# Pairing a large and a small expert per slot in a routed expert stage, with one weight load issued before the size decision

## The chip, the cores and the metric

One core of one Trainium2 chip runs the whole program. The metric is the device time of one execution in microseconds (us). Five engines work beside each other, each with its own instruction stream and its own sequencer that takes branches: TensorE (PE in the rows, with PEld for its weight loads and PEldq for its sequencer), VectorE (DVE), ScalarE (ACT), GpSimd (POOL) and SyncE (SP). SP only issues transfers and takes branches; its instructions appear as SPq.

## The reference

The program is two transformer blocks of two layers each, on 256 latent tokens of width 1024 and 256 context tokens. Each layer of the first block has a mixture of experts, and only this part is touched. Layer 0 routes 512 tokens, layer 1 routes 256:

```python
g_idx = top-1 of 4 groups;  top_i = top-2 of the 8 experts of that group
experts = g_idx * EXPERTS_PER_GROUP + top_i            # 32 experts, 2 per token
counts = jnp.bincount(e_flat, length=N_EXPERTS)        # tokens of each expert
def expert_block(a):
    xb, e = a
    return (jax.nn.silu(xb @ w1[e]) * (xb @ w3[e])) @ w2[e]
y = sum over a token's two experts of weight * expert_block(token)
```

`w1` and `w3` are 1024x512 and `w2` is 512x1024, all float32, so one expert's weights are 6 MB. How many experts are used, and how many tokens each gets, is only known at run time. On these inputs the reference's routing gives layer 0 fifteen used experts with 216, 165, 139, 138, 118, 80, 58, 53, 29, 18, 4, 3, 1, 1 and 1 tokens, and layer 1 fourteen with 133, 119, 79, 61, 56, 24, 12, 9, 8, 6, 2, 1, 1 and 1.

## The kernel before

`route_tokens` (line 764) computes, on VectorE and TensorE, the size of each expert, a rank for each (`rn`), and from the rank a slot number `uc`. It writes small tables: `meta` and `meta2` hold the expert of each slot and its token count, `gtab` the token rows of each slot for the gathers, `stabs` the rows for the scatters. Two chosen experts stand in slots 0 and 1, so that their weights can be loaded ahead.

`experts` (line 982) is one long unrolled program of turns, one per slot, with branches that every engine takes for itself on a value that it has loaded from `meta2`:

- Two turns of kind "any" for slots 0 and 1.
- Then rounds (`round_`, line 1173). Round i has a "large" turn for slot 2 + i, counted from the large end, and a "small" turn for slot 31 - i, counted from the smallest used expert up. Large means more than 64 tokens. Layer 0 has a large turn in rounds 0 to 14, layer 1 in rounds 0 to 6. Each turn stands in `If n > 0` (line 1180); where the slot is empty, the Else only transposes the rows for the next turn (`next_rows`, line 1183).
- A turn of up to 32 tokens runs a quarter block, one of 33 to 64 a half block, one of more a full block of 128 rows and, over 128 tokens, a `rest` for the further rows (line 1167, behind a branch with a prefetch hint for TensorE). Each block is a first part (w1 and w3), the transposes of the next turn's rows (line 995), and a second part (w2), then a scatter on GpSimd (line 1000).
- Ahead of a turn, `ahead` issues a gather of token rows for a later turn on GpSimd (line 722).

With the sizes above, the executed experts of layer 0 come in the order 165, 118, 216, 1, 139, 1, 138, 1, 80, 3, then 4, 18, 29, 53 and 58, each of these five behind an empty large turn: five empty turns in all, for slots 6 to 10. Layer 1 runs 61, 79, 133, 1, 119, 1, then 1, 2, 6, 8 and 9 each behind an empty large turn (slots 4 to 8), and then 12, 24 and 56, which stand in rounds without a large turn.

Weights come in six pieces of 1 MB per expert (`expert_weights`, line 977; the transfer is line 143), issued by SP, inside the `If` of the turn. They go to a ring of buffers that is handed out in program order over the unrolled turns: 16 pieces in layer 0, 18 in layer 1. Empty turns have their places in the ring too. A piece's issue waits until the turn that used its buffer has left its branch, and until the transfer before it on the same completion counter is done. After the last turn, `combine` (line 1194) loads the scattered rows back (`y`, line 1202).

Of the kernel before, what the change touches and what calls it, by code (L numbers as in the profile page):

```python
# [11 lines left out]
I32 = mybir.dt.int32  # L12
# [85 lines left out]
class Builder:  # L98
# [665 lines left out]
    def route_tokens(self, l, nt, gp, mp, rp):  # L764
# [11 lines left out]
        units = mt([NE, 2 * NE], "units")  # L776
        nc.vector.tensor_copy(units[:, 0:NE], self.iota[0:NE, 0:NE])
        nc.vector.tensor_scalar(units[:, NE:], self.iota[0:NE, 0:NE], -1.0, float(NE - 1), ALU.mult, ALU.add)
# [76 lines left out]
        rn = mt([NE, 2], "rn")  # L855
        nc.vector.tensor_reduce(rn[:, 0:1], before, AX.X, ALU.add)
        used = mt([NE, NE], "used")
        nc.vector.tensor_scalar(used, srow, 0.0, None, ALU.is_gt)
        nc.vector.tensor_reduce(rn[:, 1:2], used, AX.X, ALU.add)
        few = mt([NE, 1], "few")  # L860
        nc.vector.tensor_scalar(few, size, 64.0, None, ALU.is_le)
        nc.vector.tensor_scalar(rn[:, 1:2], rn[:, 1:2], -1.0, float(NE), ALU.mult, ALU.add)
        uc = mt([NE, 1], "uc")
        nc.vector.scalar_tensor_tensor(uc, few, rn[:, 1:2], rn[:, 0:1], ALU.mult, ALU.add)
        uh = mt([NE, 2 * NE], "uh")
        nc.vector.tensor_scalar(uh, units, uc, None, ALU.is_equal)
# [7 lines left out]
        nc.tensor.matmul(mb[0:NE, 0:2 * NE], lhsT=eix, rhs=uh, start=True, stop=True)  # L874
        mb2 = self.bankB()
        nc.tensor.matmul(mb2[0:NE, 0:2 * NE], lhsT=cnt, rhs=uh, start=True, stop=True)

        meta = keep([1, 4 * NE], "meta", I32)
        nc.vector.tensor_copy(meta[:, 0:2 * NE], mb[0:1, 0:2 * NE])
        nc.vector.tensor_copy(meta[:, 2 * NE:4 * NE], mb2[0:1, 0:2 * NE])  # L880
# [38 lines left out]
        for out, parts in ((tb, self.iota[:, 0:P]), (sb, self.cst[:, C_IOTAM:C_IOTAM + P]),  # L919
# [13 lines left out]
            if out is tb:  # L933
                tx = rows_of(tb)
                gx = mt([P, GC], "gx")
                nc.vector.tensor_scalar(gx, tb, float(T), float(T), ALU.is_gt, ALU.mult)
                gtab = keep([P, GC], "gtab", I32)
                nc.vector.scalar_tensor_tensor(gtab, tx, -1.0, gx, ALU.add, ALU.subtract)

                meta2 = keep([1, 7 * NE], "meta2", I32)  # L940
                for i in range(2):
                    c = slice(2 * NE * i, 2 * NE * i + 2 * NE)
                    nc.vector.scalar_tensor_tensor(meta2[:, c], gtab[0:1, 0:2 * NE], 0.0, meta[:, c], ALU.mult, ALU.add)
                for i, op in enumerate((ALU.is_gt, ALU.is_le)):
                    v = meta2[:, (2 + i) * NE:(3 + i) * NE]
                    nc.vector.scalar_tensor_tensor(meta2[:, (4 + i) * NE:(5 + i) * NE], v, 64.0, v, op, ALU.mult)
                nc.vector.tensor_tensor(meta2[:, 6 * NE:7 * NE - 2], meta2[:, 4 * NE + 2:5 * NE],
                                        meta2[:, 5 * NE:6 * NE - 2], ALU.add)
# [33 lines left out]
    def experts(self, l, nt, mp, first, meta, meta2, gtab, stabs, XG, XE, ybuf):  # L982
# [121 lines left out]
        turns = [("any", 0, 0), ("any", 1, 1)]  # L1104
        for i in range(NE - 2):
            turns += [("large", i, 2 + i)] * (i < most[0]) + [("small", i, NE - 1 - i)]

        def ahead(k):
            if k + AHEAD < len(turns):
                kind, _, slot = turns[k + AHEAD]  # L1110
                gather(slot * nt, XG[k % AHEAD], 64 if kind == "small" else P)

        def turn(k, n, W):

            kind, i, slot = turns[k]
            x = XT[k % 2]
            groups = nt if kind == "any" else 1 + sum(i < m for m in most[1:nt]) if kind == "large" else 1

            def block(g, size, b=lambda: None):
# [4 lines left out]
                two(slot * nt + g, W, ht)  # L1124

            def rest(g):
# [3 lines left out]
                if more:  # L1130
                    with tc.If(load(meta2 if k > 1 else meta, 2 * NE + slot, T, engines=[ENG.Pool]) > P * (g + 1)):
                        gather(slot * nt + g + 1, XE)
# [14 lines left out]
            label = f"rest{l}_{k}"  # L1147
            if groups > 1:
                tc.mark_branch_hint_location(label, "LikelyTaken", [ENG.PE])
                with tc.If(load(meta2 if k > 1 else meta, 2 * NE + slot, T, engines=[ENG.Pool]) > P):  # L1150
                    gather(slot * nt + 1, XE)
            if kind == "large":
                block(0, 0, lambda: next_rows(k))
            else:
                with tc.If(n < 33) as fewer:
                    block(0, 2, lambda: next_rows(k))
                with fewer.Else():
                    if kind == "small":
                        block(0, 1, lambda: next_rows(k))
                    else:  # L1160
                        with tc.If(n < 65) as few:
                            block(0, 1, lambda: next_rows(k))
                        with few.Else():
                            block(0, 0, lambda: next_rows(k))
            if groups > 1:
                with tc.If(n > P, label=label):
                    rest(1)

        def next_rows(k):
            if k + 1 < len(turns):  # L1170
                rows_T(XG[(k + 1) % AHEAD], XT[(k + 1) % 2], 64 if turns[k + 1][0] == "small" else P)

        def round_(i):

            for k in [k for k, t in enumerate(turns) if k > 1 and t[1] == i]:
                kind, _, slot = turns[k]
                ahead(k)
                at, e = (4 * NE + slot, slot) if kind == "large" else (5 * NE + i, NE + i)
                n = load(meta2, at, T)
                with tc.If(n > 0) as some:  # L1180
                    turn(k, n, self.expert_weights(wm, load(meta2, e, NE - 1, engines=[ENG.SP])))
                with some.Else():
                    next_rows(k)
            if i + 1 < NE - 2:
                with tc.If(load(meta2, 6 * NE + i + 1, 2 * T) > 0):
                    round_(i + 1)

        for k in range(2):
            ahead(k)
            turn(k, load(meta, 2 * NE + k, T), first[k])  # L1190
        with tc.If(load(meta2, 6 * NE, 2 * T) > 0):
            round_(0)
# [557 lines left out]
```

## Time and profile before

| quantity | value |
|---|---|
| median of 3 runs | 2325.05 us (2316.84 to 2331.53) |
| the profiled execution | 2326.15 us, its span 2324.3 us |
| mean granted TensorE clock | 0.912 |
| busy share of the span | TensorE 84%, VectorE 43%, ScalarE 32%, GpSimd 12% |
| DMA, mean over the span | 196 GB/s |
| 390 to 800 us (layer 0: routing tables and experts) | TensorE busy 304 of 410 us, clock 0.86, DMA share 0.62, 241 GB/s |
| 1035 to 1337 us (layer 1: the same) | TensorE busy 200 of 302 us, clock 0.83, DMA share 0.73, 287 GB/s |

In timeline rows a time in brackets is how long the engine sat idle before the row's first instruction, and what released it; "issue" means that it waited for nothing that the profile shows.

### The profile page before, as it was taken

The numbers are of one execution on the slowest core, as the hardware profiler recorded it, in microseconds if no ns is written. First come the engines' busy times: TensorE is split into PE (matmuls) and PEld (weight loads), VectorE is DVE, ScalarE is ACT, GpSimd is POOL, SyncE is SP. The second block draws the span as 40 slices with busy tenths as digits, with TensorE's granted clock in tenths as the row PEclk, the third lists the DMA queues.
The fourth block names the chain that finished last, engine by engine and source line by source line (L and its number), as shares of the span: only waits on it lengthen the run. The fifth ranks groups of instructions, "written<-read, shape, count | busy, mean of one in ns | idle before, by whom it ended". The sixth has DMA issues, their size and how long they took to land. (4 is left out here: it accounts for less than half of the span.)

```text
span 2324.3 us, 27711 instructions
## 1 busy us (share of the span) xinstructions
PE 1948.4 (84%) x10138; PEld 1348.4 (58%) x10138; DVE 1002.8 (43%) x1956; ACT 739.9 (32%) x1322; POOL 272.6 (12%) x214
## 2 busy tenths in 40 slices
PE   6999796778876489977865549999899899998997
PEld 3656575334433167753432237777688677776885
DVE  3346655300000174561000056656654567566554
ACT  2233431100111154411111045444444355434442
POOL 0002301101111052120111102000200020002000
PEclk9999797789997789978987769999999999998998
DMA  9974115354767762156668764344455434454550
GB/s 396 375 280 155 65 37 217 130 209 187 317 255 296 276 239 70 42 205 273 242 253 340 307 241 169 129 145 168 163 186 185 152 129 147 143 181 150 184 181 29
DMA packets 75147, 456.01 MB, mean 196 GB/s; under 512 B 13544, under 2 KB 14092, under 8 KB 24496
## 3 DMA queue, kind: packets, MB, share of 16 engines
q1 hardware_dynamic: 61632, 430.99, 49.5%
q0 software_dynamic: 9664, 14.79, 1.8%
q10 hardware_dynamic: 3632, 7.37, 0.9%
q8 instruction: 129, 2.11, 0.4%
q14 instruction: 90, 0.74, 0.1%
HBM read 455.65 MB, written 13.30 MB: 202 GB/s over the span
## 5 line engine op out<-in xcount | busy, mean ns | idle before, releaser
L167 DVE TENSOR_TENSOR whl<-w,whl 128x1024 fp32r<-128x1024 f32 x312 | 397.1, 1287 | 234.9 <-ACT whl L166 224.2
L166 ACT ACTIVATE whl<-w 128x1024 fp32r<-128x1024 f32 x332 | 344.4, 1057 | 260.5 <-PE bankA L180 208.0
L178 PE MATMUL bankA<-whl,x2h 128*128 128x512 f32 (+1 forms) x864 | 345.3, 400 | 9.6 <-ACT x2h L238 7.2
L180 PE MATMUL bankA<-whl,x2l 128*128 128x512 f32 (+1 forms) x864 | 345.0, 400 | 5.8 <-DVE x2l L239 5.8
L179 PE MATMUL bankA<-whl,x2h 128*128 128x512 f32 (+1 forms) x864 | 342.0, 397 | 0.0
L178 PEld LDWEIGHTS bankA<-whl,x2h 128*128 128x128 f32 x864 | 168.4, 195 | 43.8 <-ACT x2h L238 8.2
L180 PEld LDWEIGHTS bankA<-whl,x2l 128*128 128x128 f32 x864 | 167.4, 194 | 40.6 <-DVE x2l L239 7.2
L179 PEld LDWEIGHTS bankA<-whl,x2h 128*128 128x128 f32 x864 | 167.9, 194 | 35.0 <-issue 2.0
L1071 PE MATMUL bankA<-w,xt 128*128 128x512 f32 x320 | 153.1, 641 | 17.2 <-issue 14.7
L1018 PE MATMUL bankA<-w,xt 128*32 128x256 f32 x1216 | 97.3, 463 | 55.5 <-DMA w<-in_wmoe 32.2
L178 PE MATMUL bankA<-whl,xh 128*128 128x512 f32 (+1 forms) x336 | 132.5, 395 | 5.4 <-ACT xh L238 5.4
L179 PE MATMUL bankA<-whl,xh 128*128 128x512 f32 (+1 forms) x336 | 129.4, 385 | 5.1 <-DVE whl L167 5.1
L180 PE MATMUL bankA<-whl,xl 128*128 128x512 f32 (+1 forms) x336 | 127.8, 384 | 0.1
L414 ACT ACTIVATE p<-bankS,sm 128x256 f32<-128x256 f32 (+2 forms) x160 | 85.7, 537 | 117.6 <-DVE sm L405 59.4
L1071 PEld LDWEIGHTS bankA<-w,xt 128*128 128x128 f32 x320 | 65.0, 206 | 99.7 <-issue 98.3
L213 POOL TENSOR_TENSOR sm<-sm,mhalf 128x1 f32<-128x1 f32 (+3 forms) x32 | 32.2, 1006 | 690.9 <-DVE sm L211 679.3
L1018 PEld LDWEIGHTS bankA<-w,xt 128*32 128x32 f32 x1216 | 47.7, 131 | 102.7 <-issue 44.7
L1022 DVE TENSOR_TENSOR s<-s,bankA 64x256 f32<-64x256 f32 x19 | 8.0, 423 | 221.9 <-ACT s L1021 221.9
L1000 POOL DMA_INDIRECT ybuf<-ys,stab x34 | 34.6, 1019 | 523.6 <-ACT ys L1038 147.1
L1075 DVE TENSOR_TENSOR s<-s,bankA 128x512 f32<-128x512 f32 x10 | 6.9, 688 | 195.2 <-PE bankA L1071 181.7
L178 PEld LDWEIGHTS bankA<-whl,xh 128*128 128x128 f32 x336 | 64.2, 191 | 32.0 <-ACT xh L238 7.4
L995 PE MATMUL bankB<-cst,xg 128*128 128x128 f32 (+1 forms) x328 | 40.4, 271 | 49.8 <-issue 31.6
(456 smaller groups left out, 2982.2 us busy)
## 6 DMA issues: line engine op xcount, KB each, us to landing
w<-in_wmoe SPq DMA_DIRECT2D x174, 1024.0 KB, 12.4
w<-in_wd SPq DMA_DIRECT2D x166, 1024.0 KB, 5.1
w<-in_wmod SPq DMA_DIRECT2D x48, 1024.0 KB, 7.5
y<-ybuf SPq DMA_DIRECT2D x12, 512.0 KB, 7.7
w<-in_rows SPq DMA_DIRECT2D x5, 1024.0 KB, 4.7
w<-mrow SPq DMA_DIRECT2D x7, 512.0 KB, 8.7
fbuf<-w SPq DMA_DIRECT2D x4, 512.0 KB, 2.8
nb<-in_nabias POOLq DMA_DIRECT2D x16, 128.0 KB, 2.5
```

Source lines behind the costliest of these rows:

```text
L166: nc.scalar.activation(h, s, AF.Copy)
L167: self.low = (eng or nc.vector).tensor_tensor(lo, s, h, ALU.subtract).ins
L178: mm(out, lhsT=xh, rhs=wh, start=start, stop=False)
L179: mm(out, lhsT=xh, rhs=wl, start=False, stop=False)
L180: mm(out, lhsT=xl, rhs=wh, start=False, stop=stop)
L213: self.power = self.nc.gpsimd.tensor_tensor(r, t, self.mhalf[:, :n], ALU.pow).ins
L414: nc.scalar.activation(p[:, :n], s[i][:, :n], AF.Exp, bias=nm[:, i:i + 1], accum_out=ss[:, i:i + 1])
L995: nc.tensor.transpose(xb[:, k], xg[0:rows, (4 * i + k) * P:(4 * i + k + 1) * P], self.ident[0:rows, 0:rows])
L1000: nc.gpsimd.indirect_dma_start(out=ybuf.rearrange("r (m d) -> (r m) d", m=1 << parts), out_offset=bass.IndirectOffsetOnAxis(ap=stabs[parts ...
L1018: nc.tensor.matmul(acc[r:r + 32], lhsT=xT[:, k, 0:32], rhs=wslice(W, m, k, 256 * f, 256), start=k == 0, stop=k == KT - 1)
L1022: nc.vector.tensor_tensor(s, s, acc[64:128], ALU.mult)
L1071: nc.tensor.matmul(acc[m], lhsT=xT[:, k], rhs=wslice(W, m, k), start=k == 0, stop=k == KT - 1)
```

## The change

The slot table is built another way, and the turns follow it.

- In the table, every used expert gets its place in the order in which it runs: slots 2, 4, 6, ... are the first, slots 3, 5, 7, ... the second of a pair. A large expert and a small one share a pair while there are large ones; the remaining small ones fill the pairs two by two. On these inputs the order in which the experts run is the same as before, in slots 0 to 14 in layer 0 and 0 to 13 in layer 1. An expert of no tokens gets a slot number beyond the table. The chain of small VectorE operations between `before` and `uc` has 17 operations where it had 5; the two operations that made `units` and four behind `gtab` are gone.
- The first of a pair has no `If n > 0`: its weight transfers stand straight in SP's stream. Its blocks stand behind one decision `either` (65 tokens): the Then side is `small` (quarter or half block), the Else side is `large` (full block and rest). The "any" turns of slots 0 and 1 use the same form.
- The second of a pair is only ever small, and keeps `If n > 0` and its Else. Inside it stands a prefetch hint for TensorE that the next pair's `either` is likely taken, that is, to `large`. Slot 2 has no hint.

```diff
+        r, u, b, s, few, near, uc, t = (mt([NE, 1], f"slot{i}") for i in range(8))
+        nc.vector.tensor_reduce(r, before, AX.X, ALU.add)
+        for c, n in ((0.0, u), (64.0, b)):
+            over = mt([NE, NE], "over")
+            nc.vector.tensor_scalar(over, srow, c, None, ALU.is_gt)
+            nc.vector.tensor_reduce(n, over, AX.X, ALU.add)
         nc.vector.tensor_scalar(few, size, 64.0, None, ALU.is_le)
-        uc = mt([NE, 1], "uc")
-        nc.vector.scalar_tensor_tensor(uc, few, rn[:, 1:2], rn[:, 0:1], ALU.mult, ALU.add)
+        nc.vector.tensor_tensor(s, u, r, ALU.subtract)
+        nc.vector.tensor_tensor(t, s, b, ALU.subtract)
+        nc.vector.tensor_scalar(near, t, -1.0, None, ALU.is_lt)
...
+        nc.vector.scalar_tensor_tensor(uc, t, few, uc, ALU.mult, ALU.add)
+        nc.vector.tensor_scalar(t, size, 0.0, float(4 * NE), ALU.is_equal, ALU.mult)
+        nc.vector.tensor_tensor(uc, uc, t, ALU.add)
...
+            if kind == "small":
+                small()
             else:
-                with tc.If(n < 33) as fewer:
-                    block(0, 2, lambda: next_rows(k))
+                with tc.If(n < 65, label=f"either{l}_{k}") as fewer:
+                    small()
                 with fewer.Else():
...
+                    large()
...
-        def round_(i):
-
-            for k in [k for k, t in enumerate(turns) if k > 1 and t[1] == i]:
-                kind, _, slot = turns[k]
-                ahead(k)
-                at, e = (4 * NE + slot, slot) if kind == "large" else (5 * NE + i, NE + i)
-                n = load(meta2, at, T)
-                with tc.If(n > 0) as some:
-                    turn(k, n, self.expert_weights(wm, load(meta2, e, NE - 1, engines=[ENG.SP])))
-                with some.Else():
-                    next_rows(k)
-            if i + 1 < NE - 2:
-                with tc.If(load(meta2, 6 * NE + i + 1, 2 * T) > 0):
-                    round_(i + 1)
+        def pair(k):
+
+            ahead(k)
+            turn(k, sized(k), load(meta2, NE + k, T), self.expert_weights(wm, load(meta2, k, NE - 1, engines=[ENG.SP])))
+            ahead(k + 1)
+            n = load(meta2, NE + k + 1, T)
+            with tc.If(n > 0) as some:
+                W = self.expert_weights(wm, load(meta2, k + 1, NE - 1, engines=[ENG.SP]))
+                if k + 2 < NE and sized(k + 2) == "large":
+                    tc.mark_branch_hint_location(f"either{l}_{k + 2}", "LikelyTaken", [ENG.PE])
+                turn(k + 1, "small", n, W)
+            with some.Else():
+                next_rows(k + 1)
+            if k + 2 < NE:
+                with tc.If(load(meta2, NE + k + 2, T) > 0):
+                    pair(k + 2)
```

On SP, at the end of a large turn of the kernel before (line 1166 is the end of its rest, line 1180 its Else and then the next turn's `If n > 0`, line 143 the weight pieces):

```order
L1166 UNCONDITIONAL_BRANCH
L1180 UNCONDITIONAL_BRANCH [waits SP_sequencer_49,DMAHW2_49,DMAHW3_49,DMAHW4_49,DMAHW5_49,DMAHW6_49,DMAHW7_49]
L1094 TENSOR_LOAD meta_3280
L1180 COMPARE_AND_BRANCH
L1094 TENSOR_LOAD meta_3280
L143 ISA
L143 DMA w<-in_wmoe 128x2048 [waits DMAHW3_49,DMAHW2_49,PE_49]
```

And in the changed kernel, at the end of the second turn of a pair (line 1186 is its Else, line 1194 the test whether there is a further pair) and the start of the next pair:

```order
L1186 UNCONDITIONAL_BRANCH [waits SP_sequencer_49,DMAHW0_49,DMAHW1_49,DMAHW2_49,DMAHW3_49,DMAHW4_49,DMAHW5_49]
L1096 TENSOR_LOAD meta_3295
L1194 COMPARE_AND_BRANCH
L1096 TENSOR_LOAD meta_3295
L143 ISA
L143 DMA w<-in_wmoe 128x2048 [waits DMAHW0_49,PE_49]
...
L143 DMA w<-in_wmoe 128x2048 [waits DMAHW5_49]
L1096 TENSOR_LOAD meta_3295
L1175 COMPARE_AND_BRANCH
L1167 COMPARE_AND_BRANCH
```

The Else with waits on the completion counters (DMAHW) of the weight transfers stood behind every turn; now it stands only behind the second of a pair. The first of a pair issues its six pieces right behind the test for the pair, and its size branch (line 1175) comes after them.

On TensorE, at the start of slot 2 in the kernel before (line 1191 tests for rounds, line 1180 is `If n > 0`, line 995 the transposes of the next turn's rows, which the scheduler has laid ahead of the full block, line 1071 the full block's matmuls):

```order
L1191 COMPARE_AND_BRANCH
L1094 TENSOR_LOAD meta_3280
L1180 COMPARE_AND_BRANCH
L1746 BRANCH_PREFETCH_HINT
L995 MATMUL bankB<-cst,xg_0_3072 128x64 [waits DVE_49,DMASW7_49,PE_49,Activation_49]
L1150 UNCONDITIONAL_BRANCH
...
L1071 MATMUL bankA<-w,xt_0_3377 128x512 [waits DMAHW2_49]
L1071 MATMUL bankA<-w,xt_0_3377 128x512 x3
```

And in the changed kernel, at the same slot (line 1200 tests for pairs, line 1175 is `either`, line 1167 the test for 33 tokens, 1020 a quarter block's matmul, 1073 a full block's):

```order
L1200 COMPARE_AND_BRANCH
L1096 TENSOR_LOAD meta_3295
L1175 COMPARE_AND_BRANCH
L1167 COMPARE_AND_BRANCH
L1020 MATMUL bankA<-w,xt_0_3388 32x256 [waits DVE_49,PE_49,DMAHW2_49,Activation_49]
...
L1167 UNCONDITIONAL_BRANCH
L1755 BRANCH_PREFETCH_HINT
L1073 MATMUL bankA<-w,xt_0_3388 128x512 [waits DVE_49,DMAHW2_49,PE_49,Activation_49]
L1159 UNCONDITIONAL_BRANCH
```

A full block stood next behind the test of its turn; now the code of a quarter and of a half block lies between the test and the full block, and a branch at line 1175 leads over them.

## Rows read from the trace of the kernel before

**Rows 1.** Stretches of both expert stages: window, us, engines' busy time (instructions), PEclk, DMA share, GB/s.
```profile
1200.00:1260.00 60.00, 31.08 (x362) 15.84 (x350) 2.15 (x6) 8.56 (x21) 10.98 (x11) 0.80 0.81 316
1260.00:1330.00 70.00, 43.84 (x378) 17.92 (x378) 3.26 (x8) 5.39 (x15) 6.84 (x7) 0.78 0.89 355
```

**Rows 2.** Waits of SP's sequencer (SPq), whole run: us in total, times, longest us.
```profile
SPq L1180 <- SPq L1180: 138.8, 49, 7.6
```

**Rows 3.** The sequencers at line 1180: count, duration ns min/median/max, first and last start us.
```profile
L1180 PEldq COMPARE_BRANCH  x35: 65/68/6523, 508.5 to 1309.3; - x35
L1180 POOLq INC_SWDGE_SEM  x10: 1142/1726/2305, 695.9 to 1258.2; - x10
```

**Rows 4.** Weight loads that SP issues: start us, duration us, pieces; last, issue to landing.
```profile
657.96 0.87 SPq L143 DMA_DIRECT2D w<-in_wmoe  x2
...
682.72 9.37 SPq L143 DMA_DIRECT2D w<-in_wmoe  x6
...
769.99 7.55 SPq L143 DMA_DIRECT2D w<-in_wmoe  x6
...
1173.26 3.81 SPq L143 DMA_DIRECT2D w<-in_wmoe  x6
...
1255.65 3.65 SPq L143 DMA_DIRECT2D w<-in_wmoe  x6
...
1261.85 45.76 SPq L143 DMA_DIRECT2D w<-in_wmoe  x18
...
w<-in_wmoe SPq DMA_DIRECT2D x174, 1024.0 KB, 12.4
```

**Rows 5.** TensorE at the end of layer 0's experts: start us, us, [idle before <-releaser].
```profile
683.89 3.66 PE L1018 MATMUL bankA<-w,xt 128*32 128x256 f32 x64 [1.30 <-DVEq L1166]
689.23 1.93 PE L1035 MATMUL bankA<-w,ht 128*32 128x256 f32 x32 [0.38 <-DVE ht L1028]
...
697.52 1.09 PE L995 MATMUL bankB<-cst,xg 64*128 64x64 f32 x8 [6.35 <-issue]
...
707.19 1.93 PE L1035 MATMUL bankA<-w,ht 128*32 128x256 f32 x32 [0.38 <-DVE ht L1028]
...
761.32 9.27 PE L1046 MATMUL bankA<-w,xt 128*64 128x512 f32 x30 [5.43 <-SPq L1180]
...
778.29 1.07 PE L1046 MATMUL bankA<-w,xt 128*64 128x512 f32 x2 [1.02 <-ACT xt L997]
...
790.33 3.65 PE L1061 MATMUL bankA<-w,ht 128*64 128x512 f32 x16 [0.52 <-DVE ht L1055]
```

**Rows 6.** TensorE at the end of layer 1's experts, same columns.
```profile
1145.83 1.93 PE L1035 MATMUL bankA<-w,ht 128*32 128x256 f32 x32 [0.38 <-DVE ht L1028]
...
1174.45 3.66 PE L1018 MATMUL bankA<-w,xt 128*32 128x256 f32 x64 [1.31 <-DVEq L1166]
...
1261.85 1.07 PE L1018 MATMUL bankA<-w,xt 128*32 128x256 f32 x4 [4.78 <-DMA w<-in_wmoe]
...
1326.44 3.65 PE L1061 MATMUL bankA<-w,ht 128*64 128x512 f32 x16 [0.52 <-DVE ht L1055]
```

**Rows 7.** TensorE's branches on sizes: idle before a block; branch durations at two lines, ns.
```profile
481.92 4.35 PE L1071 MATMUL bankA<-w,xt 128*128 128x512 f32 x5 [8.00 <-issue]
...
L1161 PEldq COMPARE_BRANCH  x5: 83/229/6265, 422.2 to 1078.0; - x5
...
L1166 PEldq COMPARE_BRANCH  x12: 74/190/5711, 444.8 to 1173.3; - x12
```

**Rows 8.** VectorE in layer 0's slot table: start us, us.
```profile
399.37 0.17 DVE L858 TENSOR_SCALAR used<-bankB 32x32 f32<-32x32 f32 x1
...
400.61 0.24 DVE L866 TENSOR_SCALAR uh<-units,uc 32x64 f32<-32x64 f32 x1
```

**Rows 9.** End of layer 0's expert stage: start us, us, engine.
```profile
794.91 1.04 POOL L1000 DMA_INDIRECT ybuf<-ys,stab  x1 [12.73 <-ACT ys L1064]
...
800.14 0.81 SPq L1202 DMA_DIRECT2D y<-ybuf  x2
```

More of the change, by code (lines that the diff above doesn't have):

```diff
@@ L1103, in experts, with next_rows, turn @@
         most = [(2 * T - 2) // (n + 1) for n in (64, 128, 256, 384)]
-        turns = [("any", 0, 0), ("any", 1, 1)]
-        for i in range(NE - 2):
-            turns += [("large", i, 2 + i)] * (i < most[0]) + [("small", i, NE - 1 - i)]
+        sized = lambda k: "any" if k < 2 else "small" if k % 2 or (k - 2) // 2 >= most[0] else "large"
         def ahead(k):
[L1109 to L1115, printed above, removed]
+            if k + AHEAD < NE:
+                gather((k + AHEAD) * nt, XG[k % AHEAD], 64 if sized(k + AHEAD) == "small" else P)
+        def next_rows(k):
+            if k + 1 < NE:
+                rows_T(XG[(k + 1) % AHEAD], XT[(k + 1) % 2], 64 if sized(k + 1) == "small" else P)
+        def turn(k, kind, n, W):
+            i = (k - 2) // 2
             x = XT[k % 2]
             groups = nt if kind == "any" else 1 + sum(i < m for m in most[1:nt]) if kind == "large" else 1
+            m = meta2 if k > 1 else meta
             def block(g, size, b=lambda: None):
@@ L1123, in block @@
                 one(W, x, ht, b)
-                two(slot * nt + g, W, ht)
+                two(k * nt + g, W, ht)
             def rest(g):
@@ L1130, in rest @@
                 if more:
-                    with tc.If(load(meta2 if k > 1 else meta, 2 * NE + slot, T, engines=[ENG.Pool]) > P * (g + 1)):
-                        gather(slot * nt + g + 1, XE)
+                    with tc.If(load(m, NE + k, T, engines=[ENG.Pool]) > P * (g + 1)):
+                        gather(k * nt + g + 1, XE)
                 if g > 1:
@@ L1145, in rest, with first @@
                         rest(g + 1)
[L1147 to L1153, printed above, removed]
-            else:
-                with tc.If(n < 33) as fewer:
-                    block(0, 2, lambda: next_rows(k))
+            def first(size):
+                block(0, size, lambda: next_rows(k))
@@ new lines, in large, with small @@
+            def large():
+                label = f"rest{l}_{k}"
+                if groups > 1:
+                    tc.mark_branch_hint_location(label, "LikelyTaken", [ENG.PE])
+                    with tc.If(load(m, NE + k, T, engines=[ENG.Pool]) > P):
+                        gather(k * nt + 1, XE)
+                first(0)
+                if groups > 1:
+                    with tc.If(n > P, label=label):
+                        rest(1)
+            def small():
+                with tc.If(n < 33) as fewer:
+                    first(2)
+                with fewer.Else():
+                    first(1)
@@ L1157, in turn @@
+            if kind == "small":
+                small()
+            else:
+                with tc.If(n < 65, label=f"either{l}_{k}") as fewer:
+                    small()
                 with fewer.Else():
[L1158 to L1164, printed above, removed]
@@ L1188, in experts @@
         for k in range(2):
             ahead(k)
-            turn(k, load(meta, 2 * NE + k, T), first[k])
-        with tc.If(load(meta2, 6 * NE, 2 * T) > 0):
-            round_(0)
+            turn(k, "any", load(meta, NE + k, T), first[k])
+        with tc.If(load(meta2, NE + 2, T) > 0):
+            pair(2)
     def combine(self, l, ybuf, rw, nt, ahead, tp):
```

47 lines of the change are left out of this document (15 added, 32 removed).

## Prediction, made before the changed kernel ran

> **What bounds the kernel now.** I read the stretches first, then SP's waits, then TensorE's timeline at the end of each expert stage. Between 1200 and 1260 us, where layer 1 runs its small experts each behind an empty large turn, the core's DMA engines are busy for a share of 0.81 at 316 GB/s and TensorE for 31 of 60 us; right behind it, where no empty turn is left, it is 0.89 and 355 GB/s, though that stretch holds the tail without loads [rows 1]. So these stretches hang on weight loads, and with empty turns the loads come slower. The reader should see why in SP's waits: the Else of an empty turn costs SP 138.8 us in 49 waits, in which it waits at line 1180 until all transfers in flight have landed [rows 2]. Then the next six pieces are issued to idle queues. There are ten empty turns, five in each layer (the ten levelling instructions of GpSimd at that line are theirs) [rows 3].
>
> The price shows in the bursts. In layer 0 five bursts of six pieces start between 682.72 and 769.99, 21.8 us apart; in layer 1 five start between 1173.26 and 1255.65, 20.6 us apart; then 18 pieces follow with no drain in 45.76 us, 17 gaps of 2.69 us, or 16.2 us for an expert [rows 4]. TensorE pays too: behind a short block it goes idle for 6.35 us with "issue" as the reason, while its branch at line 1180 takes up to 6523 ns to jump over the code of an empty turn, against a median of 68 ns where it doesn't jump [rows 3, 5].
>
> **The change, part by part.** The order of the experts stays, so everything ahead of slot 2's decision differs only by the slot table, and the gain lies in the ends of the two stages.
>
> *Layer 0, experts 3, 4, 18, 29, 53 and 58.* They take from 683.89 to 790.33 + 3.65 = 793.98, 110.1 us [rows 5]. Now there is no drain between them. First the weights alone: the last pieces of the 3-token expert are issued at 657.96, and the 80-token expert holds TensorE from there to 683.89. Before, the next burst had to wait until 682.72, since the empty turn's six places in the ring are used up; in the changed kernel its pieces need only an expert three turns back to be over. With 12.4 us from issue to landing, 30 pieces end at 657.96 + 0.87 + 12.4 + 30 x 2.69 = 752, against 769.99 + 7.55 + 12.4 = 790 [rows 4]. Then TensorE alone. A warm quarter block is 7.3 us (683.89 to 689.23 + 1.93); a cold one with its transposes 11.6 (697.52 to 707.19 + 1.93); a half block from its first long stretch to the next 17.0 (761.32 to 778.29), the last one 15.7 with its short waits (778.29 to 793.98) [rows 5]. The first of a pair, when small, ends with a jump over its unused `large` code, about twice as far as the jump into `large`; nearest are the jumps over an empty turn, 6.4 us [rows 3, 5], and I take that for slots 10 and 12. Sum: 7.3 + 8.4 (a warm quarter with transposes) + 6.4 + 11.6 + 10 (between warm and cold) + 6.4 + 17.0 + 15.7 = 82.8, so TensorE is done 27.3 us earlier, at 766.7. It is later than the weights at 752, so **-27**; were the jumps free, the weights would decide, and with some 6 us of last block it is -36.
>
> *Layer 1, from the expert behind the 119-token one.* Its weights waited until 1173.26; in a ring of 18 pieces they now need the expert three back, which ends at 1145.83 + 1.93 = 1147.8, so they land under the 119-token expert: one expert's 16.2 us of loading gone from the end. The four bursts after it take 16.2 us in place of 20.6 each [rows 4, 6]: 17.6. Together **-34**. TensorE does not object: from 1174.45, eight quarters at about 9.5, one half at 17, one far jump of 6.4 and three jumps over shorter code at 2 are 105 us, ending at 1280, while the weights let it end at 1326.44 + 3.65 - 34 = 1296 [rows 6].
>
> *The decision `either`.* A large expert behind a small block's code needs a jump of TensorE into `large`. Rows give both ends: unhinted, the same decision left TensorE idle for 8.00 us, its branch took 6265 ns; the hinted branch into `rest` took 190 ns in the median, 5711 at worst [rows 7]. Slots 0 and 1 had two such jumps in a row before and have one now: nothing. Slot 2 is new and has no hint: 6.4 in each layer. Slots 4, 6 and 8 of layer 0 and 4 of layer 1 are hinted: 1 us each, nearer the median, between 0.2 and 6.4. Layer 0 **+9.4** (7 to 26), layer 1 **+7.4** (6.6 to 13). In these stretches TensorE is behind nothing else, so this delays all that follows.
>
> *The slot table.* 12 more dependent VectorE operations stand ahead of the gathers, and TensorE waits for the table. Five of them took 1.24 us (399.37 to 400.61) [rows 8], so **+3.0** in each layer (2 to 3). The operations removed were not on this path.
>
> *GpSimd at the end of layer 0.* Its last expert is now the first of a pair, so behind its scatter come the levelling of the taken branch, one more gather (slot 17), the Else of slot 15 and the end of the pair. In the kernel before, 5.2 us lie between the last scatter and the `y` loads [rows 9]. I add two levellings at the median of 1.7 [rows 3] and 1.04 for the gather, taken like a scatter [rows 9]: **+4.5**, between 2 and, if a levelling waits for the gather to land, 12. Layer 1 ends on the second of a pair, as before: nothing. Also at nothing: the gathers and levellings of the ten empty turns, hidden under the weight waits; without that cover they would cost 1.7 each, and they only go away.
>
> **Sum.** Layer 0: -27.3 + 9.4 + 3.0 + 4.5 = -10.4. Layer 1: -33.8 + 7.4 + 3.0 = -23.4. Together -33.8, from the profiled 2326.15 to 2292.4; the median before is 1.1 lower, so **2291**.
>
> [...]
>
> **Rivals.**
>
> *A, the jumps are cheap.* For: most branches at lines 1161 and 1166 take 0.2 us [rows 7]. Against: the far jumps at line 1180 took 6.4 us each in layer 0. Layer 0 -36 + 0.8 + 3 + 4.5 = -28; layer 1 -33.8 + 0.4 + 3 = -30; together -58: **2267**.
>
> *B, the jumps eat the gain.* Every jump into `large` costs 6.4, hint or not. For: 5711 ns at a hinted branch [rows 7]. Layer 0 -27.3 + 25.6 + 3 + 4.5 = +5.8; layer 1 -33.8 + 12.8 + 3 = -18; together -12: **2313**, and 2320 with GpSimd's end at 12. No change that a measurement can tell.
>
> *C, the other side: wrong hints.* At slots 10, 12 and 14 of layer 0 and 6, 8, 10 and 12 of layer 1 the hint says `large` and a small expert comes. If the hint then fetches `large`'s code in place of the code that follows, each such turn starts with another 6.4. On top of B, layer 0 has +19.2; in layer 1 TensorE's 105 us become 131, plus 13 if the three shorter jumps cost 6.4 as well, and it passes the weights at 122: +9 to +22. Together -12 + 28 to +41: 2341 to **2354**. It makes the kernel slower from 4 us apiece, and only where B holds too. Against: nothing in the trace shows a wrong hint, and a hinted branch that isn't taken, for a small `rest`, cost little in the median.
>
> *D, the change doesn't do what it says.* The Else of the second of a pair still drains, but it is only reached when the pair is half empty, at the very end; against it stands SP's order. I give it nothing of its own.
>
> **Chances.** My forecast 0.44 (its own range 2278 to 2304), A 0.24, B 0.22, C 0.10. The range takes in A with a faster end and B with GpSimd's slow end: 2258 to 2320; C and the far ends are left out. A measurement of this kernel tells about 1% from no change: faster is below 2302, slower above 2348. Faster has A and nearly all of the forecast, 0.66; slower half of C, 0.06; the rest is 0.28.
>
> **What the changed profile should show.** SP: no waits on itself at the Else of a turn between slots 2 and 14, pieces 2.7 us apart through the ends of both stages. TensorE: idle "issue" of about 6 us ahead of slot 2's full block and behind the small first turns of slots 10 and 12, and about 1 us ahead of slots 4 to 8. Layer 0's last block ends 10 to 18 us earlier, layer 1's stage is some 23 us shorter by its own start. I am wrong if the hinted jumps cost as much as the unhinted, if a small turn starts late behind a wrong hint, or if the pieces come at the old pace for another wait.

## The result, and the profile after

The changed kernel took 2292.03 us (median of 4, 2286.6 to 2297.46), against 2326.72 for the kernel before in the same rounds: a ratio of 0.9856, with a 95% interval of 0.9813 to 0.9898. The forecast was 2291. The profiled execution has a span of 2292.1 us against 2324.3, 32.2 less.

I cut both timelines at the same places: the first matmul that counts tokens (the stage's start), the end of the last full block (the 80-token expert in layer 0, the 119-token one in layer 1), the end of the last expert, and the first `y` load. This is the table against which each step is held; the later kernels stand in it too. The times of the stretches are differences of starts and ends in TensorE's and SP's timeline, from one profiled execution of each kernel; executions of one kernel differ by up to 13 us (e5, 2297.12 to 2310.11), so a few us between two medians tell nothing.

| kernel | median us | ratio to before in the same rounds, 95% | layer 0: start to 80 | to last end | to `y` | layer 1: start to 119 | to last end |
|---|---|---|---|---|---|---|---|
| before | 2326.72 | | 285.6 | 111.4 | 6.2 | 135.1 | 157.0 |
| after | 2292.03 | 0.9856 [0.9813, 0.9898] | 292.4 | 82.7 | 11.2 | 148.9 | 128.2 |
| e1, no hint on the decision | 2288.25 | 0.9842 [0.9805, 0.9879] | 292.3 | 82.3 | 10.4 | 149.3 | 128.1 |
| e2, large side first | 2302.29 | 0.9901 [0.9861, 0.9940] | 288.5 | 102.6 | 10.5 | 152.2 | 123.0 |
| e3, old rounds, none empty | 2264.34 | 0.9739 [0.9699, 0.9779] | 285.9 | 84.2 | 6.1 | 137.3 | 123.9 |
| e4, drain put back | 2339.92 | 1.0068 [1.0043, 1.0094] | 292.1 | 106.4 | 10.5 | 148.7 | 153.7 |
| e5, first of a pair in an If | 2303.06 | 0.9907 [0.9874, 0.9940] | 289.0 | 100.2 | 11.0 | 149.0 | 126.0 |
| e6, gather moved into the If | 2290.17 | 0.9843 [0.9789, 0.9897] | 292.5 | 82.7 | 10.8 | 148.7 | 126.9 |
| e7, mixed order | 2269.0 | 0.9757 [0.9716, 0.9798] | 278.2 | 86.3 | 10.5 | 142.6 | 122.9 |
| e8, hint in the quarter block | 2286.09 | 0.9831 [0.9790, 0.9872] | 287.2 | 82.2 | 10.6 | 148.9 | 123.0 |
| e9, e5 without the hint | 2289.89 | 0.9839 [0.9810, 0.9868] | 297.0 | 84.7 | 10.3 | 148.4 | 123.1 |
| e10, after, code moved by 140 | 2309.85 | 0.9930 [0.9907, 0.9954] | 299.3 | 92.9 | 10.6 | 154.4 | 132.9 |
| e11, e7, code moved by 140 | 2283.13 | 0.9804 [0.9763, 0.9846] | 289.2 | 97.0 | 10.4 | 138.3 | 123.4 |
| e12, after, code moved by 68 | 2299.43 | 0.9888 [0.9850, 0.9926] | 285.8 | 101.8 | 10.8 | 146.9 | 124.1 |

From before to after: +6.8, -28.7 and +5.0 in layer 0, +13.8 and -28.8 in layer 1, -31.9 in all, and -0.3 in what lies around.

The stretches of layer 1's end, as in [rows 1]:

```profile
1200.00:1260.00 60.00, 39.58 (x495) 21.49 (x494) 3.57 (x10) 8.35 (x20) 8.01 (x8) 0.86 1.02 407
1260.00:1302.00 42.00, 24.58 (x166) 9.99 (x166) 1.83 (x4) 3.69 (x8) 4.01 (x4) 0.80 0.64 260
```

The first goes from a share of 0.81 and 316 GB/s to 1.02 and 407 GB/s; the second is short because the stage ends there.

SP's waits, whole run, as in [rows 2]: of the 138.8 us of SP on itself at empty turns 8.3 are left, at the second of the last pair, and it now waits for pieces to land and for the turns that hold the ring:

```profile
SPq L143 <- DMA w<-in_wmoe: 146.5, 63, 7.5
SPq L143 <- PEq L1163: 94.4, 4, 29.5
...
SPq L1186 <- SPq L1186: 8.3, 2, 5.9
```

The weight loads, as in [rows 4] (last line: the median from issue to landing):

```profile
691.57 60.06 SPq L143 DMA_DIRECT2D w<-in_wmoe  x26
...
1173.11 96.23 SPq L143 DMA_DIRECT2D w<-in_wmoe  x42
...
w<-in_wmoe SPq DMA_DIRECT2D x174, 1024.0 KB, 15.0
```

In layer 1 42 pieces go out in one run; by the trace the first lands at 1178.15 and the last at 1289.56, 2.72 us each. In layer 0 26 pieces start at 691.57, which is where the 80-token expert ends, and the last lands at 767.72.

TensorE at the ends, as in [rows 5] and [rows 6], first layer 0, then layer 1:

```profile
714.91 5.01 PE L1020 MATMUL bankA<-w,xt 128*32 128x256 f32 x64 [6.27 <-issue]
...
726.85 2.63 PE L1020 MATMUL bankA<-w,xt 128*32 128x256 f32 x32 [2.44 <-DMA w<-in_wmoe]
...
743.33 9.93 PE L1048 MATMUL bankA<-w,xt 128*64 128x512 f32 x32 [6.20 <-issue]
...
760.95 7.09 PE L1048 MATMUL bankA<-w,xt 128*64 128x512 f32 x32 [1.66 <-ACT ys L1066]
...
770.54 3.65 PE L1063 MATMUL bankA<-w,ht 128*64 128x512 f32 x16 [0.52 <-DVE ht L1057]
```

```profile
1196.21 3.68 PE L1020 MATMUL bankA<-w,xt 128*32 128x256 f32 x35 [5.60 <-DMA w<-in_wmoe]
...
1266.21 5.83 PE L1020 MATMUL bankA<-w,xt 128*32 128x256 f32 x60 [4.56 <-DMA w<-in_wmoe]
...
1285.08 10.08 PE L1048 MATMUL bankA<-w,xt 128*64 128x512 f32 x32 [9.39 <-issue]
...
1297.54 3.65 PE L1063 MATMUL bankA<-w,ht 128*64 128x512 f32 x16 [0.52 <-DVE ht L1057]
```

The decisions on size, as in [rows 7], are idle times ahead of a full block (slots 1, 2, 6 and 8 of layer 0, slot 4 of layer 1) and the sequencer's branch at that line:

```profile
478.25 15.92 PE L1073 MATMUL bankA<-w,xt 128*128 128x512 f32 x32 [8.20 <-issue]
...
505.52 15.67 PE L1073 MATMUL bankA<-w,xt 128*128 128x512 f32 x32 [1.92 <-issue]
...
618.67 6.67 PE L1073 MATMUL bankA<-w,xt 128*128 128x512 f32 x11 [5.40 <-issue]
...
665.79 16.24 PE L1073 MATMUL bankA<-w,xt 128*128 128x512 f32 x32 [4.77 <-issue]
...
1148.01 15.55 PE L1073 MATMUL bankA<-w,xt 128*128 128x512 f32 x32 [6.65 <-issue]
...
L1175 PEldq COMPARE_BRANCH  x17: 77/405/7035, 428.1 to 1259.8; - x17
```

The slot table on VectorE, as in [rows 8], and the first `y` load with TensorE's branch at the end of the pairs, as in [rows 9]:

```profile
401.44 0.17 DVE L857 TENSOR_SCALAR over<-bankB 32x32 f32<-32x32 f32 x1
...
404.82 0.23 DVE L875 TENSOR_SCALAR uh<-cst,slot 32x32 f32<-32x32 f32 x1
```

```profile
785.37 0.81 SPq L1211 DMA_DIRECT2D y<-ybuf  x2
...
L1194 PEldq COMPARE_BRANCH  x15: 71/71/4249, 564.5 to 1302.0; - x15
```

### The profile page after: what moved, and what is told of

It is laid out like the page before. It is cut to its first block, busy times and chain, and to the rows that moved or that the text cites. A ratio compares the mean times of both kernels' runs of the same rounds, so it can differ in the third digit from the quotient of the medians.

```text
span 2292.1 us, 27169 instructions
## 1 busy us (share of the span) xinstructions
PE 1927.0 (84%) x10066; PEld 1342.1 (59%) x10066; DVE 1005.3 (44%) x1968; ACT 732.4 (32%) x1304; POOL 263.3 (11%) x205
## 5 line engine op out<-in xcount | busy, mean ns | idle before, releaser
L180 PE MATMUL bankA<-whl,xl 128*128 128x512 f32 (+1 forms) x336 | 128.2, 385 | 0.1
L1020 PE MATMUL bankA<-w,xt 128*32 128x256 f32 x1216 | 86.4, 428 | 48.8 <-issue 25.4
L1088 PE MATMUL bankA<-w,ht 128*128 128x512 f32 x160 | 71.3, 599 | 7.8 <-DVE ht L1082 7.8
```

Of the source, the lines that this page charges most:

```text
L180: mm(out, lhsT=xl, rhs=wh, start=False, stop=stop)
L1020: nc.tensor.matmul(acc[r:r + 32], lhsT=xT[:, k, 0:32], rhs=wslice(W, m, k, 256 * f, 256), start=k == 0, stop=k == KT - 1)
L1088: nc.tensor.matmul(yb[m], lhsT=hT[:, k], rhs=w2slice(W, k, m * 512, 512), start=k == 0, stop=k == 3)
```

## The experiments

**Is it the drain?** e4 puts one back, with no branch: `drain(k, W)` behind the six pieces of each small expert of the two ends.

```diff
+        def drain(k, W):
+            if k >= (10 if l == 0 else 6):
+                nc.sync.dma_start(dry, W[5][0:1, 0:64])
```

> The changed kernel with a drain put back: behind the six pieces of each expert of slots 10 to 14 in layer 0 and 6 to 13 in layer 1 SP issues a transfer of 256 bytes out of the last piece, which waits until that piece has landed, and what stands behind it in the queue waits too. No branch is added. Theory (the weight loads bound the ends of both stages): the bursts go from 16.2 to about 21 us each; layer 0 loses some 15 us, layer 1 some 28: 2325 to 2340. Rival (TensorE's jumps are what mattered, the drain lay beside them): under 6 us, 2292 to 2298.

SP's wait at the new line, and two bursts of layer 0 around one of the small transfers:

```profile
SPq L1184 <- DMA w<-in_wmoe: 193.0, 13, 18.3
...
701.19 3.26 SPq L143 DMA_DIRECT2D w<-in_wmoe  x6
723.02 0.28 SPq L1184 DMA_DIRECT2D dry<-w  x1
724.99 3.59 SPq L143 DMA_DIRECT2D w<-in_wmoe  x6
```

The bursts are 23.8 us apart here. The ends become 23.7 and 25.5 us longer, 49 of the 57.5 us that they had gained. (The dose is not the same: e4 has 13 such waits, the kernel before ten empty turns with its bursts 21.8 us apart.) So the drain is the cause, and TensorE's jumps over empty turns had cost little that the loads did not cover. The rival with the jumps alone is out.

**What does the rest of the change cost?** e3 takes the kernel before and leaves out the empty turns, by a capacity that only these inputs allow.

```diff
+        most[0] = nt
         turns = [("any", 0, 0), ("any", 1, 1)]
```

> The kernel before with only as many rounds with a large turn as these inputs need (four in layer 0, two in layer 1), so that no large turn is empty; it holds for these inputs only. It has the old table, no new decision and no small code ahead of large code. Theory: the empty turns cost 36 us at the end of layer 0 (the weights then decide, since no far jump is left) and some 33 at the end of layer 1, and the pairing itself only costs: 2256, between 2250 and 2266. Rival: the gain of the changed kernel is TensorE's jumps over empty turns alone, and the drain of SP's queue lay beside other work: 21.8 us in layer 0 and 8 in layer 1, so 2296.

It is 28 us faster than the changed kernel. Against before, the ends lose 27.2 and 33.1 us, and little is added ahead of them (0.3 and 2.2). Layer 0's end is as long as in the changed kernel although no jump over large code stands in it (the longest idle time on "issue" there is 3.62 us); TensorE waits for weights instead:

```profile
719.25 3.64 PE L1018 MATMUL bankA<-w,xt 128*32 128x256 f32 x32 [3.88 <-DMA w<-in_wmoe]
723.93 3.63 PE L1018 MATMUL bankA<-w,xt 128*32 128x256 f32 x28 [1.04 <-DMA w<-in_wmoe]
...
762.06 5.35 PE L1061 MATMUL bankA<-w,ht 128*64 128x512 f32 x16 [0.52 <-DVE ht L1055]
```

**Are the jumps into large code paid, and does the hint help?** e1 leaves out the hint on the decision, e2 also exchanges the two sides, so that large code is fallen into.

```diff
-                if k + 2 < NE and sized(k + 2) == "large":
-                    tc.mark_branch_hint_location(f"either{l}_{k + 2}", "LikelyTaken", [ENG.PE])
...
-                with tc.If(n < 65, label=f"either{l}_{k}") as fewer:
-                    small()
-                with fewer.Else():
-                    large()
+                with tc.If(n > 64) as more:
+                    large()
+                with more.Else():
+                    small()
```

> The changed kernel without TensorE's hint on the next pair's size decision (the hint on the rest stays). In the changed kernel the three hinted jumps into the large code of layer 0 took 5.6, 4.7 and 4.6 us and the one of layer 1 took 5.1 us on TensorE's sequencer. [...] Rival 1: the hint already saves a part, and each jump becomes some 6.5 to 7 us as the unhinted one of slot 1 is: 2298 to 2300. [...]

> The changed kernel with the two sides of the size decision exchanged: the large code stands behind the test and is fallen into, the small code stands behind it and is jumped to; no hint on the decision. Theory: the jumps into large code are on the path, since TensorE is the bound where large experts run; slot 1 gains 6.7 us in layer 0 and 7.0 in layer 1, slots 6 and 8 of layer 0 4.7 and 4.6, slot 4 of layer 1 5.1, slot 4 of layer 0 little, because its weights come late. A small first of a pair pays its far jump at its start in place of its end, as often as now, but for slot 14 of layer 0, where it comes onto the path: +6. Together some -20: 2265 to 2278. [...]

Without the hint nothing moves, in time or in the table, and the four jumps that had it take 4.6 to 5.4 us, within the 4.5 to 7 us and the 2292, give or take 6, that I expected if the hint is of no use: in this kernel it does no good. e2, at 2302, lies above its theory and also above the 2285 to 2295 that I had expected if the cost only moves, to other branches or to the weights: layer 0 up to the 80-token block is 3.9 us shorter, but its end is 19.9 us longer. TensorE in e2, at slots 10 and 12 and at the last two experts:

```profile
706.22 3.63 PE L1020 MATMUL bankA<-w,xt 128*32 128x256 f32 x31 [6.76 <-issue]
711.66 3.55 PE L1020 MATMUL bankA<-w,xt 128*32 128x256 f32 x33 [1.80 <-issue]
...
734.79 4.17 PE L1020 MATMUL bankA<-w,xt 128*32 128x256 f32 x36 [7.69 <-DMA w<-in_wmoe]
...
750.34 9.85 PE L1048 MATMUL bankA<-w,xt 128*64 128x512 f32 x32 [4.55 <-issue]
...
770.85 9.65 PE L1048 MATMUL bankA<-w,xt 128*64 128x512 f32 x32 [4.57 <-issue]
```

The jump to the small side is paid at the start of slots 10, 12 and 14 (6.76, 7.69 and 4.57 us idle, the second until a weight piece lands), and at slot 10 a second pause of 1.80 us follows within straight code. Slot 10 starts 20.6 us behind the 80-token block, against 8.6 in the changed kernel; the rest of the 19.9 is not taken apart here.

**Mixed order.** e7 takes the large side first only where large experts can be expected, and has no hint on the decision.

```diff
+                if 0 < k <= 2 * nt:
+                    with tc.If(n > 64) as more:
+                        large()
+                    with more.Else():
+                        small()
+                else:
...
```

> The changed kernel with the large side first for slots 1 to 8 in layer 0 and 1 to 4 in layer 1, where large experts can be expected, and the small side first for slot 0 and for the later slots; no hint on the decision. Any sizes still run rightly. With the large side first everywhere, layer 0 up to the end of the 80-token block was 3.8 us shorter than in the changed kernel, the ends of both stages lost what it gained, and layer 1 lost by slot 0, which is small. Theory: the gain of the one and the ends of the other add up: layer 0 -4, layer 1 -5 to -7: 2281, between 2276 and 2287. Rival (code that is fallen into after a jump stalls later by as much): 2288 to 2296.

2269.0: more than both said, since layer 0 up to the 80-token block is 14.2 us shorter, not 4. Slot 8's full block, where the changed kernel pauses for 4.77 us and then takes 16.24 us:

```profile
649.65 13.97 PE L1073 MATMUL bankA<-w,xt 128*128 128x512 f32 x32 [0.23 <-DMA w<-in_wmoe]
```

The block itself is 2.3 us shorter. The granted clock in the block is 1.00 from 650 to 663 us here. In the changed kernel, behind the pause, it is 0.88 from 666 to 682 us: 0.51 up to 670 us and 1.00 from there. So the changed kernel loses 4.77 us ahead of this block and 2.3 more in it; what lowered the clock, no run shows.

**A hint that nothing crosses.** e8 puts the half block ahead of the quarter block and the hint at the head of the quarter.

```diff
             if kind == "small":
-                small()
+                with tc.If(n > 32) as more:
+                    first(1)
+                with more.Else():
+                    if k + 1 < NE and sized(k + 1) == "large":
+                        tc.mark_branch_hint_location(f"either{l}_{k + 1}", "LikelyTaken", [ENG.PE])
+                    first(2)
```

> The changed kernel with the half block first and the quarter block second in the second of a pair, so that a quarter block ends with no jump over a half block, and the hint on the next pair's decision stands at the head of the quarter block, behind the jump to it. Theory (a hint is lost when a taken branch over other code comes between it and its branch): the hinted jumps of slots 4, 6 and 8 in layer 0 and 4 in layer 1 fall from some 5 us to under 1.5; slot 4 of layer 0 gains little, since its weights are late; each quarter start pays 0.3 to 3 us for the jump over the half block: -4 to -12, 2280 to 2288. Rival (a hint ahead of this decision has no effect wherever it stands): the jumps stay at 4.5 to 5.6 us and the time at 2290 to 2300.

```profile
L1180 PEldq COMPARE_BRANCH  x17: 68/378/6775, 426.9 to 1253.5; - x17
```

Of the four hinted jumps, only slot 8's fell, to 0.44 us; slots 4 and 6 took 5.1 and 5.2, layer 1's slot 4 took 4.95. The theory that a branch in between loses the hint doesn't hold; why slot 8 fell is open. The time, 2286, lies in the theory's range, but it is only 2 us from e1, which has no hint at all, so it doesn't tell.

**Loading ahead of the decision.** e5 puts the first of a pair back into an `If n > 0`, weights and all; e9 is e5 without the hint (as in e1).

```diff
+            n = load(meta2, NE + k, T)
+            with tc.If(n > 0) as some:
+                turn(k, sized(k), n, self.expert_weights(wm, load(meta2, k, NE - 1, engines=[ENG.SP])))
+            with some.Else():
+                next_rows(k)
```

> The changed kernel with the first of a pair put back into an If on its token count, weights and all, with its Else; the pairs, the table and the size decision stay. The first of an executed pair is never empty on these inputs, so the Else is never taken. Theory (the gain comes from there being no empty turn in the program's path, not from loading ahead of a decision): SP takes one more branch of 0.03 us and one more load of a value of 0.3 us per pair, TensorE jumps once more over a short Else: 2292, between 2286 and 2300. Rival (loading ahead of the decision brings a part itself, since the count has to be read before the six pieces go out): 2300 to 2310.

> The kernel with the first of a pair in an If, now without TensorE's hint on the next pair's decision. With the hint it took 2303 us: its weight loads at the end of layer 0 ran at the pace of the changed kernel (last piece issued 60.6 us after the 80-token block, against 59.7), but TensorE stood for 7.6 us with no releaser in the middle of the straight matmuls of slots 10 and 12, at which the hint had named the large side and a small expert came. [...]

e5 was slower, as its rival said, but not for its reason: SP's last piece goes out some 60 us behind the 80-token block in both kernels. TensorE stands still in the middle of slots 10 and 12:

```profile
693.11 1.49 PE L1020 MATMUL bankA<-w,xt 128*32 128x256 f32 x21 [0.25 <-issue]
702.24 5.00 PE L1020 MATMUL bankA<-w,xt 128*32 128x256 f32 x43 [7.64 <-issue]
...
735.08 5.33 PE L1020 MATMUL bankA<-w,xt 128*32 128x256 f32 x44 [7.60 <-issue]
```

I expected e9 at 2284 to 2292, without these pauses, if the wrong hint makes them, and at 2298 to 2308, with them, if the place of the code does. In e9 the pause at slot 10 is short, layer 0's end is 84.7 and the time 2290:

```profile
708.49 2.53 PE L1020 MATMUL bankA<-w,xt 128*32 128x256 f32 x41 [1.57 <-issue]
```

So with the hint gone the kernel with the If is no slower than the changed one: that the first of a pair loads ahead of its decision brings nothing that shows; that there is no empty turn does. The pauses go with the wrong hint, though e9's code also lies some instructions elsewhere than e5's. All traces together bear it out: within straight matmuls there are eight pauses of 7.1 to 8.9 us with "issue" as the reason, in e5, e10 and e12, each in a small first of a pair whose hint had named the large side; the five kernels without that hint (e1, e2, e7, e9, e11) have none above 4.0. It takes more than the hint, since the changed kernel itself, e4, e6 and e8 have it and none above 3.9.

**The end of layer 0.** e6 moves one gather.

```diff
-            ahead(k + 1)
             n = load(meta2, NE + k + 1, T)
             with tc.If(n > 0) as some:
+                ahead(k + 1)
```

> The changed kernel with the gather that stands ahead of the second of a pair moved into its If, so that an empty second issues none. In the changed kernel 11.2 us lie between the end of layer 0's last block and the first load of y, against 6.2 in the kernel before. Theory: the last levelling of GpSimd waits for that gather to land (issued 777.74, landed 781.60, the wait over at 783.23); without it 7 to 8.5 us lie there, and the time is 3 to 4 us less, 2288 (too little to tell by time). Rival: the levellings themselves, at 1.3 us each, and TensorE's jumps at the end make the distance: 10 to 11 us stay.

```profile
766.48 3.65 PE L1063 MATMUL bankA<-w,ht 128*64 128x512 f32 x16 [0.52 <-DVE ht L1057]
...
780.92 0.81 SPq L1211 DMA_DIRECT2D y<-ybuf  x2
```

10.8 us stay between the end of the last block and the `y` load: the gather was not the cause. In the changed kernel TensorE's own branch there takes up to 4249 ns (above); it is over at 783.01, GpSimd's wait at 783.23, and in e6 the two are at 778.35 and 778.81. That the jumps make the whole of the 5 us is argued from this, not shown by a run.

**Does it matter where the code lies?** e10 and e12 only add 35 and 17 tiny matmuls ahead of layer 0's first transposes; e11 adds 35 to e7.

```diff
+        if l == 0:
+            pad = self.bankB()
+            for _ in range(35):
+                nc.tensor.matmul(pad[0:1, 0:1], lhsT=self.ident[:, 0:1], rhs=self.ident[:, 0:1], start=True, stop=True)
         rows_T(XG[0], XT[0])
```

> The changed kernel with 35 tiny matmuls more on TensorE ahead of layer 0's first transposes, where it waits 4 us for a gather; they move all later TensorE code by 140 instructions, so that slot 10's code lies as in the kernel with the If on the first of a pair (two instructions off), and change nothing else. Theory (placement alone makes the stalls): TensorE stands for some 7 us within slot 10's matmuls, perhaps slot 12's, layer 0's end goes from 82.7 to 88 to 100 us, 2297 to 2307. Rival (the hint or the If makes them): layer 0's end stays at 81 to 85, 2290 to 2295.

> The changed kernel with 17 tiny matmuls more in the same place, a shift of 68 instructions. [...] Rival (the tiny matmuls themselves or the wait behind them cost, not the shift): 2300 to 2302, half of what 35 cost, with the jumps at 0.4 and 5 us as in the changed kernel.

> The kernel with the mixed order of the two sides (2269 us), with 35 tiny matmuls more on TensorE ahead of layer 0's first transposes, which move its later code by 140 instructions. In the changed kernel the same shift cost 18 us (2310 against 2292), by jumps of slots 0 and 2 that had taken 0.4 us and then took 6.6 and 7.9. [...] Rival (the 2269 was a lucky place): 2280 to 2295.

Moving the code by 140 instructions costs the changed kernel 18 us. Slots 0 and 2 of layer 0 pause now, whose jumps took 0.4 us before, while slot 1's falls from 6.7 us to 1.9:

```profile
430.06 15.62 PE L1073 MATMUL bankA<-w,xt 128*128 128x512 f32 x32 [7.35 <-issue]
...
507.43 12.76 PE L1073 MATMUL bankA<-w,xt 128*128 128x512 f32 x24 [9.37 <-issue]
```

The pauses of e5 within slots 10 and 12 of layer 0 did not come back, so e10's theory had about the size (3 us above its range) and not the place. But such pauses stand in layer 1, within slots 6, 8 and 10, at which the hint is wrong too:

```profile
1209.71 3.15 PE L1020 MATMUL bankA<-w,xt 128*32 128x256 f32 x25 [7.50 <-issue]
...
1242.93 2.72 PE L1020 MATMUL bankA<-w,xt 128*32 128x256 f32 x18 [7.06 <-issue]
...
1273.84 4.50 PE L1020 MATMUL bankA<-w,xt 128*32 128x256 f32 x53 [8.92 <-issue]
```

In e12, with 68 instructions, the jumps of slots 0, 1 and 2 all take 0.4 us and layer 0 is 6.6 us shorter up to the 80-token block; but its end is 19.1 longer, with e5's pauses in slots 10 and 12 again:

```profile
698.99 4.88 PE L1020 MATMUL bankA<-w,xt 128*32 128x256 f32 x42 [8.06 <-issue]
...
732.89 4.48 PE L1020 MATMUL bankA<-w,xt 128*32 128x256 f32 x35 [8.40 <-issue]
```

e12's time lies in the 2285 to 2312 that I expected if the cost of a jump goes with where the code lies, and it is close to half of what 35 tiny matmuls cost, as its rival said; the jumps rule the rival out, and slot 0's first matmul stands 31.1 us behind the stage's start, against 30.9 without the 17. So the place of the code changed both: within blocks with a wrong hint the pauses were 7.1 to 8.9 us in e10 and e12 and not above 3.9 in the changed kernel, and slot 2's jump took 0.4 us or 7.9. e7 loses 14 us by the same 140, which is its rival's range, and not the under 10 that I expected if the order of the sides makes most of the gain; still, the mixed order is 23 us ahead of the small side first in the one place and 27 in the other. The mixed order has no hint: against e1, also without it, it is 19 us ahead, and in the other place, where e10 pays for the wrong hint in layer 1, no run tells order and hint apart. Which distances are dear was not settled.

## Why the prediction was right, point by point

**The end of layer 0, -27 by TensorE: right size, wrong owner.** I had the weights land at 752 and TensorE end later, at 766.7. The part that failed is the ring: I let all 30 pieces follow on the 3-token expert's. Only the first four can; the other 26 need the 80-token turn to end, as the burst at 682.72 did in the kernel before, and start at 691.57 in the changed one. They take 60.06 us to issue, the last lands at 767.7, and the last block ends 6.5 us after that, at 774.2. The weights decide, to within some 2 us: TensorE's far jumps (6.27 and 6.20 us idle) lie in the gaps that they leave (the second ends at 743.33, and slot 13's third weight piece, which its block needs at once, lands at 743.96), and e3, without those jumps, has nearly the same end. The -36 that rival A had for free jumps was never to be had. e5 shows how near TensorE is to deciding all the same: with two more pauses of 7.6 us, and 11.0 us idle ahead of slot 13 in place of 6.2, its last piece lands 24 us before the end, and the end is 17.5 us later.

**The end of layer 1, -34: mechanism right, 5 us too much.** The loads did what was said: they let TensorE end at 1296, I wrote; the last piece landed at 1289.6, and a block needs some 6.5 us behind it. But ahead of the last half block TensorE pauses for 9.39 us, two far branches in a row (4.8 and 5.2 us), at the end of the quarter before it and over its own quarter, and ends at 1301.2. I had priced three such jumps at 2 us each and hidden them. e3, without the first of them, has the -33.1.

**The decision, +9.4 and +7.4: the sizes the wrong way round.** Slot 2, unhinted, was to pay 6.4 us and paid 0.4 (1.92 us idle, against 1.67 before); slots 6 and 8 were to pay 1 for their hint and paid 5.40 and 4.77 of idle time, and slot 4's jump took 5.6 us beside weights that came as late; slot 4 of layer 1 paid 6.65. Layer 0 up to the 80-token block came out at +6.8, where the decision and the table had +12.4; the errors have opposite signs. In layer 1 some 5.7 more lie between slot 0's first matmul and slot 1's, and no term had that: 4.2 of it inside slot 0's half block (13.79 us before, 17.99 now, at a granted clock of 0.95 and 0.81), and 1.5 in idle time ahead of slot 1, where slot 0's jump over its unused large code and the jump into slot 1's, 5.5 and 7.0 us, stand in place of 5.7 and 2.8. In layer 0 slot 0's `rest` became 7.7 us shorter (451.84 to 473.92 before, 455.66 to 470.04 now, at a granted clock of 0.77 and 1.00), which no term had either. Its half block, before and now:

```profile
456.15 9.96 PE L1046 MATMUL bankA<-w,xt 128*64 128x512 f32 x32 [2.81 <-issue]
```

```profile
456.85 7.09 PE L1048 MATMUL bankA<-w,xt 128*64 128x512 f32 x32 [0.31 <-ACT xt L999]
```

e3 with the old code has 3.09 us idle there. So it comes with the new code's shape or place; which of the two is not shown.

**The table, +3.0 each:** 3.38 us in place of 1.24 (401.44 to 404.82), so +2.1 in layer 0, and TensorE's wait for it grew by 1.7 in layer 1. The 12 operations cost 0.18 us each, less than the 0.25 that I took from five.

**GpSimd at the end of layer 0, +4.5:** +5.0 measured, but for another reason than its gather (e6).

**Rivals.** A's price for the drain held in layer 1 (-33.8; e3 has -33.1) and not in layer 0 (-36; e3 has -27.2), and its cheap jumps were wrong. That e3 is 61.6 us faster, near A's 58, doesn't bear A out, since e3 has neither the table nor the decisions that A's sum pays for. B's price for the hinted jumps was right, and its sum failed by slot 2 and layer 0's first slots. C, the wrong hint, cost nothing in this kernel (e1), and 7 to 9 us at three slots each in e5 and e10 and at two in e12; it comes within the block, though, not at its start as C had it.

That 2291 met 2292 owes something to chance: a neutral move of the code makes 2299 or 2310 of it, and three terms were off by 3 to 6 us, with both signs. Layer 0 came out at -16.9 where I had -10.4, layer 1 at -15.0 where I had -23.4. One of my signs of being wrong came true, the hinted jumps that cost as much as the unhinted; and layer 0's last block ended 19.8 us earlier, not 10 to 18.

## What to carry to other kernels

An untaken turn was not free here, where its Else has to level the queues (without empty turns SP's waits there went from 138.8 us to 8.3, and the drain that e4 put back made the two ends 49 us longer): look for waits of a queue's engine on itself, and price them by the pace of the loads with and without them. Where loads refill a ring, write down for every burst which turn frees its places before letting it run on. Here the order with the likely side fallen into (e7) was 19 us ahead of e1, and fallen into everywhere (e2) it was 14 behind: in branchy code on one engine try the order turn by turn, and measure a second placement of the code, which alone made 7 to 18 us here (e12, e10), before believing a gain of under 1%. A hint on a branch that often goes the other way gave nothing here (e1) and cost 7 to 9 us at a slot in other placements (e5, e10, e12).

## What the runs showed of the hardware that I had not expected

- TensorE's jump over the small code of a turn took between 0.4 and 7.9 us without a hint, and between 0.4 and 5.6 with one; slot 2's, unhinted, went from 0.4 to 7.9 us when the code moved by 140 instructions.
- Pauses of 7.1 to 8.9 us without a releaser stood within straight matmul code, 11 to 46 matmuls into a block at which the hint had named the other side (e5, e10, e12). What made them, no run shows.
- Behind a pause of 4.77 us a full block took 16.24 us at a granted clock of 0.88 (0.51 from 666 to 670 us, then 1.00), against 13.97 at 1.00 without the pause (e7).
